# An ifftshift of an 8192 x 8192 matrix: from sixteen quadrant DMAs to sixty-four whole-row DMAs

## The chip, the cores and the metric

One core of one Trainium2 chip runs the kernel. The metric is the device time of one execution in microseconds (us). A profiled execution has a span too, from its first to its last recorded instruction; the time on the device is a little longer than the span.

## The reference

```python
def setup_inputs():
    return {
        "x": np.random.randn(8192, 8192).astype(np.float32),
    }

def reference(x: np.ndarray) -> np.ndarray:
    return np.fft.ifftshift(x)
```

Both sides are even, so the shift is by half in each direction: output element (r, c) is input element ((r + 4096) mod 8192, (c + 4096) mod 8192). Nothing is computed; the four quadrants change places diagonally. The matrix has 268.4 MB, which are read once and written once. A row has 32 KiB, half a row 16 KiB.

## The kernel before

The kernel has no tiles and no compute. It moves the data from DRAM to DRAM by DMAs that SyncE (SP) issues, and SP issues nothing else. `quads` (lines 23 to 28) lists for each quadrant of the output its rows and columns and the rows and columns of the input that belong there. The outer loop (line 33) goes over the four quadrants, top left, top right, bottom left, bottom right; the inner one (line 36) cuts each into four pieces of 1024 rows. So there are 16 DMAs, each of 1024 half rows, 16 MiB.

In each DMA both sides have the same pattern: 1024 runs of 16 KiB, one run every 32 KiB, so that every other 16 KiB of both matrices is skipped. The skipped halves belong to another quadrant and are moved by a DMA four places later or earlier. Each DMA reports its end by 16 increments of its semaphore, and the packets of the trace lie on 16 DMA engines. If the 1024 rows are dealt to the engines in equal runs of neighbouring rows, an engine has 64 rows of each DMA, and the pieces of neighbouring engines begin 64 x 32 KiB = 2 MiB apart.

The order is that of the program: SP issues the DMAs one after the other on its one queue. The framework hands out eight semaphores for these DMAs in turn, so the ninth DMA and each after it waits until the DMA eight places earlier has landed. No two DMAs touch the same output bytes, and there is no other dependence. At the end SP waits for the last DMAs, and a closing barrier (recorded at line 70) ends the program. The four memsets recorded at line 59 belong to the framework.

Of the kernel before, what the change touches and what calls it, by code (L numbers as in the profile page):

```python
# [1 line left out]

# [4 lines left out]


@with_exitstack  # L10
def kernel(
    ctx: ExitStack,
    tc: tile.TileContext,
    x: bass.AP,
    out: bass.AP,
):
    nc = tc.nc

    R, C = x.shape
    hr = R // 2  # L20
    hc = C // 2

    quads = [
        ((0, hr), (0, hc), (hr, R), (hc, C)),
        ((0, hr), (hc, C), (hr, R), (0, hc)),
        ((hr, R), (0, hc), (0, hr), (hc, C)),
        ((hr, R), (hc, C), (0, hr), (0, hc)),
    ]

    engines = [nc.sync]  # L30
    nsplit = 4
    k = 0
    for (or0, or1), (oc0, oc1), (ir0, ir1), (ic0, ic1) in quads:
        rows = or1 - or0
        step = rows // nsplit
        for s in range(nsplit):
            a = s * step
            b = a + step
            eng = engines[k % len(engines)]
            k += 1  # L40
            eng.dma_start(
                out=out[or0 + a : or0 + b, oc0:oc1],
                in_=x[ir0 + a : ir0 + b, ic0:ic1],
            )


# [1 line left out]
_INS = ['x']  # L48
_OUTS = [((8192, 8192), 'float32')]


def kernel(**inputs):
    import numpy as _np
    import concourse.bacc as _bacc
    import concourse.tile as _tile
    from concourse import mybir as _mybir
    from concourse.bass_utils import run_bass_kernel_spmd as _run

    nc = _bacc.Bacc("TRN2", target_bir_lowering=False, num_devices=1)  # L59
    arrays, args = {}, []  # L60
    for name in _INS:
        a = _np.ascontiguousarray(inputs[name])
        if a.dtype.kind in "iu":
            a = a.astype(_np.int64)
        arrays[f"in_{name}_dram"] = a
        args.append(nc.dram_tensor(f"in_{name}_dram", a.shape, _mybir.dt.from_np(a.dtype), kind="ExternalInput").ap())
    for i, (shape, dtype) in enumerate(_OUTS):
        dt = _mybir.dt.from_np(_np.dtype(dtype))
        args.append(nc.dram_tensor(f"out_{i}_dram", shape, dt, kind="ExternalOutput").ap())
    with _tile.TileContext(nc) as tc:  # L70
        kernel(tc, *args)
    r = _run(nc, [arrays], core_ids=[0])
    got = tuple(r.results[0][f"out_{i}_dram"] for i in range(len(_OUTS)))
    return got[0]
```

## Time and profile before

| | |
|---|---|
| median of 4 runs | 814.69 us (813.1 to 816.67) |
| the profiled execution, time | 814.51 us |
| the profiled execution, span | 812.7 us |
| DMAs issued | 16, of 16384 KB each |
| DMA packets | 16640: 16384 of data and 256 short ones |
| bytes under way | 268.44 MB read, 268.44 MB written |
| compute engines | POOL 0.2 us, all others nothing |

The profile has no compute to read. What remains is the DMA part: a line of tenths that says how busy the core's 16 DMA engines were in each of 40 slices of the span, a line with the rate in each slice (counted once per byte moved, though each byte is read and written), the sum over the queue, and the DMA issues with their median time from issue to landing. 16384 data packets for 268.44 MB are packets of 16 KiB: each run of half a row is one packet. The 256 short ones are 16 for each DMA, the semaphore increments.

### The profile page before, as it was taken

The numbers are of one execution on the slowest core, as the hardware profiler recorded it, in microseconds if no ns is written. First come the engines' busy times: TensorE is split into PE (matmuls) and PEld (weight loads), VectorE is DVE, ScalarE is ACT, GpSimd is POOL, SyncE is SP. The second block draws the span as 40 slices with busy tenths as digits, with TensorE's granted clock in tenths as the row PEclk, the third lists the DMA queues.
The fourth block names the chain that finished last, engine by engine and source line by source line (L and its number), as shares of the span: only waits on it lengthen the run. The fifth ranks groups of instructions, "written<-read, shape, count | busy, mean of one in ns | idle before, by whom it ended". The sixth has DMA issues, their size and how long they took to land. (4 is left out here: it accounts for less than half of the span.)

```text
span 812.7 us, 61 instructions
## 1 busy us (share of the span) xinstructions
POOL 0.2 (0%) x4
## 2 busy tenths in 40 slices
POOL 0000000000000000000000000000000000000000
DMA  9999999999999999999999999999999999999998
GB/s 297 327 314 330 331 334 323 333 323 333 332 335 326 337 333 334 331 335 340 331 333 335 331 335 328 335 334 331 331 333 336 338 333 332 334 335 335 331 336 295
DMA packets 16640, 268.44 MB, mean 330 GB/s; under 512 B 256, under 2 KB 256, under 8 KB 256
## 3 DMA queue, kind: packets, MB, share of 16 engines
q1 hardware_dynamic: 16640, 268.44, 99.2%
HBM read 268.44 MB, written 268.44 MB: 661 GB/s over the span
## 5 line engine op out<-in xcount | busy, mean ns | idle before, releaser
L59 POOL MEMSET const-uint8-127<- 128x1 uint8 x1 | 0.1, 103 | 0.0
L59 POOL MEMSET const-bfloat16-1.0<- 128x1 bf16 x1 | 0.1, 102 | 0.0
L59 POOL MEMSET const-float32-1.0<- 128x1 f32 x1 | 0.1, 100 | 0.0
L59 POOL MEMSET const-float32-0.0<- 128x1 f32 x1 | 0.1, 99 | 0.2 <-issue 0.2
## 6 DMA issues: line engine op xcount, KB each, us to landing
out_dram<-in_x_dram SPq DMA_DIRECT2D x16, 16384.0 KB, 157.7
```

Of the source, the lines that this page charges most:

```text
L59: nc = _bacc.Bacc("TRN2", target_bir_lowering=False, num_devices=1)
```

## The change

The loop over quadrants is replaced by a loop over blocks of 128 output rows, in order from the top. One DMA writes a block whole: 128 rows of 32 KiB, 4 MiB without a gap. It reads the 128 input rows that lie half the matrix away. Within a row the source begins at the second half (`+ hc`) and steps back by half a row (`[-hc, 2]`) to the first. There are 64 DMAs instead of 16, all still issued by SP in one line.

```diff
+ROWS_PER_DMA = 128
...
-    engines = [nc.sync]
-    nsplit = 4
-    k = 0
-    for (or0, or1), (oc0, oc1), (ir0, ir1), (ic0, ic1) in quads:
-        rows = or1 - or0
-        step = rows // nsplit
-        for s in range(nsplit):
-            a = s * step
-            b = a + step
-            eng = engines[k % len(engines)]
-            k += 1
-            eng.dma_start(
-                out=out[or0 + a : or0 + b, oc0:oc1],
-                in_=x[ir0 + a : ir0 + b, ic0:ic1],
-            )
+    for row in range(0, R, ROWS_PER_DMA):
+        src = (row + hr) % R
+        nc.sync.dma_start(
+            out=bass.AP(
+                out.tensor,
+                out.offset + row * C,
+                [[C, ROWS_PER_DMA], [hc, 2], [1, hc]],
+            ),
+            in_=bass.AP(
+                x.tensor,
+                x.offset + src * C + hc,
+                [[C, ROWS_PER_DMA], [-hc, 2], [1, hc]],
+            ),
+        )
```

An access pattern lists, from the outside in, pairs of step and count, in elements. In the built program the destination stands as 256 runs of 4096 elements one behind the other, the source as 128 rows of two runs with a step of -4096. The contiguous run stays half a row, 16 KiB, on both sides. With equal shares of neighbouring rows an engine now has 8 rows of a DMA, 16 runs, and the pieces of neighbouring engines begin 8 x 32 KiB = 256 KiB apart. The eight semaphores are handed out as before, so from the ninth DMA on each waits for the one eight places earlier; 56 of 64 DMAs have such a wait, where 8 of 16 had it.

More of the change, by code (lines that the diff above doesn't have):

```diff
@@ L21 @@
     hc = C // 2
[L23 to L28, printed above, removed]
-    engines = [nc.sync]
-    nsplit = 4
-    k = 0
-    for (or0, or1), (oc0, oc1), (ir0, ir1), (ic0, ic1) in quads:
-        rows = or1 - or0
-        step = rows // nsplit
-        for s in range(nsplit):
-            a = s * step
-            b = a + step
-            eng = engines[k % len(engines)]
-            k += 1
-            eng.dma_start(
-                out=out[or0 + a : or0 + b, oc0:oc1],
-                in_=x[ir0 + a : ir0 + b, ic0:ic1],
-            )
+    for row in range(0, R, ROWS_PER_DMA):
[12 more added lines that the diff above has]
+        )
 _INS = ['x']
```

## The prediction

> **What bounds the kernel now.** I read the page first: the slices, the queue and the HBM line.
>
> ```profile
> DMA  9999999999999999999999999999999999999998
> GB/s 297 327 314 330 331 334 323 333 323 333 332 335 326 337 333 334 331 335 340 331 333 335 331 335 328 335 334 331 331 333 336 338 333 332 334 335 335 331 336 295
> ...
> q1 hardware_dynamic: 16640, 268.44, 99.2%
> HBM read 268.44 MB, written 268.44 MB: 661 GB/s over the span
> ```
>
> The 16 DMA engines are busy in every slice and 99.2% of the span. Only the first and last slice fall below 310 GB/s, because they hold the start and the end. So no gap can be closed; time changes only if a packet takes longer or shorter.
>
> Next, SP's line and its waits, to see whether issuing ever limits the transfers.
>
> ```profile
> L41 SPq DMA_DIRECT2D out_dram<-in_x_dram x16: 578/49485/95256, 0.7 to 653.6; - x16
> ...
> DMA to landing us min/median/max: 54.9/157.7/200.0
> ```
>
> The shortest issue took 578 ns; the median of 49,485 ns is SP held back by a full queue, since a DMA of 16.8 MB takes 16.8/330 = 50.8 us to move. Landing 157.7 us after the issue means about three DMAs queued ahead. SP is far ahead of the data; the last issue begins at 653.6 us.
>
> Third, windows of 5 us around the place where one DMA gives way to the next. The second DMA's 16 increments arrive from 105.2 to 106.6 us.
>
> ```profile
> core 0: us, POOL busy (x), PEclk, DMA share, GB/s
> 95.00:100.00 5.00, 0.00 (x0) 1.00 0.97 318
> 100.00:105.00 5.00, 0.00 (x0) 1.00 1.01 338
> 105.00:110.00 5.00, 0.00 (x0) 1.00 1.00 328
> 110.00:115.00 5.00, 0.00 (x0) 1.00 0.98 328
> ```
>
> The window with the handover, 105 to 110, has a share of 1.00 and 328 GB/s, like its neighbours: a boundary between DMAs costs nothing visible.
>
> Last, the packet records themselves. The 16384 data packets of 16 KiB took 787 ns in the mean, 740 in the median, 608 at the least; 32% took 615 or less, 1% over 1341. Packets follow each other on an engine with about 2 ns between. So an engine alone moves a packet in 608 ns, and the other 179 ns are what reading and writing with 15 others costs. The span adds up: 1024 packets per engine x 0.787 = 806.0, about 2.3 us until the first packet, 1024 x 2 ns = 2.3 between packets, the rest of 2.1 for uneven ends and the closing barrier: 812.7. I write it as 1024 m + 6.7.
>
> One more reading carries the estimate. I put the data packets in order of start and cut them into 1024 rounds of 16 (the 16 engines finish each DMA within 2 us, so a round is nearly one packet of each). Numbering the rounds by eights, the mean duration by place in the eight is 758, 777, 767, 795, 820, 806, 786, 789 ns, each with a standard error of 6.4 ns; the first and the second half of the run show the same rise in the middle. Eight rounds are 8 x 32 KiB = 256 KiB of address in each engine. So what a packet costs depends on where the engines stand in the matrix, by about 4% each way.
>
> **The change part by part.** *SP's issues, 16 to 64.* At the two unhindered durations, 578 and 652 ns, 64 issues are 37 to 42 us of SP, against 800 us of transfer: hidden behind the queue. The new period is 4.19 MB/330 GB/s = 12.7 us, twenty times an issue. If that cover were gone the worst is 48 x 0.65 = 31 us.
>
> *The waits.* From the ninth DMA on each issue waits for the DMA eight earlier; queued behind it on SP are only the later DMAs, and the engines are the ones who would wait for those. While it waits seven DMAs, 7 x 12.7 = 89 us, are queued. The queue held about three DMAs of 65 packets per engine, and eight of 17 packets (136) are fewer than that. Price 0. Without that cover each later DMA would show the time from issue to first packet, 2.09 - 0.73 = 1.36 us.
>
> *Semaphore packets.* 48 more per engine at 9 ns, on the path: +0.4 us.
>
> A page that speaks against the change, weighed here: the Trainium skill, "DMA: Bandwidth & Descriptors", section "Anatomy of one DMA", puts a fixed cost of about 2.0 us on each DMA (fitted on the GpSimd path), mostly the receipt of the last write; 48 more in series would be +96 us by an estimate from that page. The handover window at 1.00 share does not show it, so the sum has 0.4 us here.
>
> *The first and the last packet.* The first DMA still needs about 1.4 us to its first packet, and the last packets still end unevenly by a packet or so. 0.
>
> *The address pattern.* This is the only large term. Packet size (16 KiB), count (16384), engines (16) and bytes stay. What changes: an engine writes its piece without gaps instead of every other 16 KiB; the two halves of a row are moved in neighbouring packets, where before they were four DMAs, some 200 us, apart; and the engines stand 256 KiB apart, no longer 2 MiB. The trace of before has no packet with the new pattern, so m is bounded by its own places: if all went as in the best place of the eight, m = 758, if all as in the worst, 820. The outer rows are the means of eight successive rounds, 736 at the lowest and 894 at the highest, 764 to 811 for nine tenths of them. The floor of 608 for every packet would need 16 engines that do not disturb each other, which no stretch approaches.
>
> I take m = 777. That is the shortest mean over one of the 16 DMAs (the thirteenth and the fifteenth; the sixteen run from 813 in the first down to 777), so a value this stream holds for 50 us. I choose the fast side because each difference removes something that can only cost: skipped bytes between two runs, and a second visit to the same rows. I do not go to 758, because 661 GB/s of reads and writes may leave little room.
>
> A page on the same point: in "DMA: Bandwidth & Descriptors", section "Latency and other measured facts", the Trainium skill reports copies between HBM tensors at 207 GB/s with a row pitch of 512 KiB, 164 at 2 MiB and 214 with a padded pitch. Read as the distance between engines, which its rows need not be, it would free 1 - 164/214 = 23% by an estimate from that page, some 625 us. The trace's 330 GB/s per direction at 2 MiB is above every one of its figures, so I do not use it.
>
> *The sum.* 1024 x 0.777 = 795.6, + 6.7 + 0.4 = 802.7 span. The profiled execution took 814.51 for a span of 812.7, 1.8 more, and the median is 0.2 above that: 804.7 us, 10 below 814.69.
>
> **The rivals.** *Slower by collisions in the new pattern (0.36).* The place is each packet's 179 ns over the floor. For it: the duration moves with the position inside 256 KiB, and that is now exactly the distance between engines and the length of a piece, so all 16 start each DMA in the same place; an engine that is one packet ahead is 16 KiB away and no longer 32; and within one DMA of before all reads lie in one half of the rows and all writes in the other, which the new order mixes. Against: before too all engines started alike, 2 MiB being a multiple of 256 KiB. Price: the mean of the four slower places, (820 + 806 + 786 + 789)/4 = 800 ns, gives 819.2 + 7.1 + 2.0 = 828 us; the worst place 820 gives 849. It decides from m = 789 on, where 1024 m is 2 us above today.
>
> *No change (0.08).* If the 661 GB/s are the limit whatever the order, only the 0.4 us remain: 815 us. For it: the 100-us rates from 200 us on are all 332 to 335. Against: the places in the eight.
>
> *The queue runs dry between smaller DMAs (0.05).* If the wait on the eighth DMA back left the engines without work, 48 x 1.36 = 65 us: 880. The 89 us of queue speak against it.
>
> *The change doesn't do what it says (0.01).* If source and destination of different shape were dealt to 8 engines, 2048 packets x 608 ns = 1245 us at least. If the contiguous destination became packets of 32 KiB, half of the 2.3 us between packets would go: 813.
>
> **How the numbers follow.** The forecast, faster, has 0.50; its own range is 785 (m = 758) to 812. About 0.3%, 2.4 us, is what a measurement of this kernel can tell from no change. Faster 0.50, within 0.3% 0.08, slower 0.36 + 0.05 + 0.01 = 0.42. The range goes up to 849 (m = 820) and leaves out 0.08 of the collision rival, the dry queue and the wrong engines; down it goes to 775, about halfway between 785 and the 763 that the fastest eight rounds (736) would give, and leaves out 0.04.
>
> **What would show it.** 17408 packets (16384 of 16 KiB, 1024 short) show that packets and engines are unchanged. A DMA share of 99% with the rate alone moved, near 334 GB/s, confirms that only m moved; a share below 97% with dips every 12.7 us would be the dry queue. Landing about 8 x 12.6 = 100 us after issue shows the depth. The rise in the middle of the eight rounds should change its shape. The prediction is wrong if m comes out above 787, and wrong in kind if the time lies in gaps.

## The result and the profile after

The changed kernel takes 814.52 us (median of 52 runs, 813.02 to 815.86), the kernel before 815.58 us (median of 79 runs). The ratio is 0.9985 with a 95% interval of 0.9976 to 0.9994: faster by 0.15%, inside the 0.3% that the prediction calls no change. The forecast was 804.7 us. The profiled execution has a span of 812.2 us, against 812.7.

The page of the changed kernel, much the same lines as were shown of before:

```profile
DMA  8999999999999999999999999999999999999998
GB/s 304 329 330 332 332 328 334 332 334 327 334 334 335 330 330 339 328 333 334 330 333 332 334 332 333 332 331 339 330 326 333 335 331 332 331 338 329 330 338 290
DMA packets 17408, 268.44 MB, mean 331 GB/s; under 512 B 1024, under 2 KB 1024, under 8 KB 1024
...
q1 hardware_dynamic: 17408, 268.44, 99.6%
HBM read 268.44 MB, written 268.44 MB: 661 GB/s over the span
```

The engines are as full as before, and the joint rate of reads and writes is again 661 GB/s. There are 17408 packets, 16384 of data and 64 x 16 short ones, so the packets are what they were; the order of the addresses and the number of DMAs are new.

SP's line in the same trace, with the time of one issue and from issue to landing:

```profile
L31 SPq DMA_DIRECT2D out_dram<-in_x_dram x64: 596/11820/28919, 0.7 to 730.1; - x64
...
DMA to landing us min/median/max: 15.3/80.0/94.5
```

An unhindered issue still takes 0.6 us. The median of 11.8 us is the full queue again, close to the 12.7 us that a DMA of 4.19 MB needs. Landing after 80 us means that some six DMAs lie in the queue. It never runs dry.

The packet records say where the forecast went. A data packet took 789 ns in the mean (787 before), the floor is 608 again, and 28% took 615 or less (32% before). What is not packets, span minus 1024 means, fell from 6.6 to 4.1 us. Put in rounds of 16 and numbered by eights, the means are 782, 774, 796, 786, 782, 786, 806, 801 ns, each with a standard error of about 5 ns: the pattern over the eight places is flatter and lies elsewhere, and its mean is nearly the same. So, as far as one trace of each kernel tells, the single packets did react to the new addresses, and the sum did not.

### The profile page after: what moved, and what is told of

It reads as the page before. It is cut to its first block, busy times and chain, and to the rows that moved or that the text cites. A ratio compares the mean times of both kernels' runs of the same rounds, so it can differ in the third digit from the quotient of the medians.

```text
span 812.2 us, 109 instructions
## 1 busy us (share of the span) xinstructions
POOL 0.2 (0%) x4
## 2 busy tenths in 40 slices
DMA packets 17408, 268.44 MB, mean 331 GB/s; under 512 B 1024, under 2 KB 1024, under 8 KB 1024
## 3 DMA queue, kind: packets, MB, share of 16 engines
q1 hardware_dynamic: 17408, 268.44, 99.6%
```

## Experiments

Every ratio is against runs of the kernel before on the same chip. Those took 823.7 to 826.5 us in the median, 1% more than the runs above, so the times below are not compared with those above.

The traces name neither the engine nor the address of a packet. Every distance between engines below rests on what was assumed for the kernel before: that the entries of a DMA's outermost dimension, here rows, are dealt to the engines in equal runs of neighbours. The runs with 8, 12 and 14 engines fit that, since the row count sets how many engines work, but they don't show which rows each engine gets.

### Half of the change at a time

`quad_128rows` keeps the quadrants and takes over the small DMAs:

```diff
-    nsplit = 4
...
+        for step in [128] * 32:
```

> One part of the change alone: DMAs of 128 rows (engines 256 KiB apart, 128 DMAs of 2 MiB), but quadrants as before, every other 16 KiB. Theory 'shared limit' (16 engines together get about 661 GB/s of reads plus writes, whatever the order; a packet takes what is left to it): within 0.5% of before, ratio 0.995 to 1.005. Rival 'two effects cancel' (the near halves gain, the short distance between engines loses): slower, ratio 1.01 or more, since here only the loss is in. Small DMAs leave the queue dry: over 850 us and a DMA share under 97%.

Measured: 1.0001 [0.9973, 1.0030]. 128 DMAs instead of 16 and 256 KiB between engines instead of 2 MiB cost nothing.

`whole_1024rows` keeps the whole rows and takes back the distance of 2 MiB between engines, with 1024 rows a DMA:

```diff
-ROWS_PER_DMA = 128
+ROWS_PER_DMA = 1024
```

> The other part alone: whole rows with the source stepping back, but 1024 rows a DMA, so that the engines stand 2 MiB apart as before (8 DMAs of 32 MiB). Shared limit: ratio 0.995 to 1.005. Two effects cancel: faster, ratio 0.99 or less, since here only the gain is in.

Measured: 1.760 [1.747, 1.773]. Neither theory allowed for this: whole rows alone are not faster but slower by three quarters. So it isn't two effects of like size that cancel either; the two parts of the change don't add.

`engines_32KiB_apart` deals the rows of a quadrant out in turn:

```diff
+                    [[C, 16], [16 * C, step // 16], [1, hc]],
```

> Quadrants and DMA sizes of before, but the rows are dealt out in turn: neighbouring engines stand one row, 32 KiB, apart, and an engine steps 512 KiB from packet to packet. Shared limit: ratio 0.99 to 1.01. A pattern-sensitive packet time (places in the eight worth 758 to 820 ns): a change of more than 1.5% one way or the other.

Measured: 1.0004 [0.9964, 1.0043]. Its packets have a mean of 806 ns in a profiled execution with a span of 832.8 us (834.6 us on the device, 1% above the median of this run), and 35% of them took 615 ns or less. Sixty-four times less distance shows no change.

`engines_16MiB_apart` uses the other end. It exchanges the halves of the rows and leaves out the shift by rows:

```diff
+                    [[R // 16 * C, 16], [C, 64], [1, hc]],
```

> Half rows as before, but an engine has 512 neighbouring rows of the whole matrix, so that neighbouring engines stand 16 MiB apart on both sides. The shift by rows is left out (an output row holds the same input row with its halves exchanged). Shared limit whatever the order: ratio 0.99 to 1.01. Pattern-sensitive packet time: slower by 5% or more, the packet mean over 830 ns, the floor unchanged at 608.

Measured: 2.619 [2.602, 2.637], the packet mean 2079 ns, the floor still 608. So order can cost a great deal, though here the missing row shift differs as well as the distance. The rates that several orders share, near 330 GB/s per direction, look like a ceiling, and the bad orders fall below it; the next runs test that.

### What the ceiling is: fewer engines, and one direction alone

The pieces are cut so that the rows of nearly all of them divide by 8, 12 or 14 and by nothing larger up to 16, for example for twelve:

```diff
+        for step in [996, 996, 996, 996, 108, 4]:
```

> Quadrants as before, cut into pieces of 1016 and 1048 rows, which can be dealt evenly to 8 engines and not to 16. Shared limit: 8 engines are under it, each packet comes near the floor of 608 to 611 ns, so 2048 x 0.611 + 7 = about 1258 us. Rival 'own pace' (a copy from DRAM to DRAM costs an engine 787 ns a packet whatever the others do): 2048 x 0.789 + 7 = about 1623 us.

> Quadrants as before, nearly all in pieces of 996 rows, which can be dealt to 12 engines. Shared limit: 12 engines at the floor would move 12 x 26.8 = 322 GB/s, just under the 330 seen, so 1365 packets each; between 840 us (all at the floor) and 900 us, packet mean 611 to 650 ns. Own pace: 1365 x 0.789 = 1084 us.

> Pieces of 1022 rows, dealt to 14 engines. At the floor they would move 375 GB/s. Shared limit: the 330 GB/s hold with two engines fewer, 812 to 830 us, packet mean about 690 to 700 ns in place of 787. Own pace: 1170 x 0.789 + 7 = 930 us.

Measured: 1249.5 us with 8 engines (1.514 [1.505, 1.523]), 837.9 with 12 (1.015 [1.011, 1.019]), 870.6 with 14 (1.055 [1.050, 1.059]). Windows of the three traces, in the order 8, 12, 14 engines; the last two columns are the busy share of 16 engines and the rate:

```profile
100.00:200.00 100.00, 0.00 (x0) 1.00 0.50 216
400.00:500.00 100.00, 0.00 (x0) 1.00 0.50 216
```

```profile
100.00:200.00 100.00, 0.00 (x0) 1.00 0.75 321
400.00:500.00 100.00, 0.00 (x0) 1.00 0.76 324
```

```profile
460.00:480.00 20.00, 0.00 (x0) 1.00 0.88 325
820.00:840.00 20.00, 0.00 (x0) 1.00 0.50 216
840.00:860.00 20.00, 0.00 (x0) 1.00 0.50 215
```

With 8 engines each packet takes 611 ns (99.9% of them 615 or less), with 12 the mean is 612: twelve engines move 642 GB/s of reads and writes over the span without getting in each other's way, and are 1.5% slower than sixteen. Engines 13 to 16 add next to nothing. That is the ceiling, and it is not an engine's own pace. (The time itself, 837.9 us, came out just under the expected 840 to 900.)

Fourteen engines reach the same 325 GB/s but end later than twelve; the expectation of 812 to 830 us missed. The ceiling is not shared evenly there: of the 14 increments of the second DMA, 6 arrive at 93 to 95 us and 8 at 117. The lucky six run through all that SP has queued and then stand idle, at the end and several times before it. The page shows the dips:

```profile
DMA  7888888888788888867888888688888868878754
...
q1 hardware_dynamic: 16640, 268.44, 81.5%
```

Fourteen engines at work throughout would give 87.5%. In windows of 5 us the share falls to 0.53 or less for 100 us in all after the start, 820 to 865 us among them. There only eight are at work, at 216 GB/s, and all their packets after 824 us take 611 ns: it was the others that had slowed them, not something of their own. By an estimate from these numbers 100 us at 216 in place of 325 GB/s lose 34 us, about the 33 us by which fourteen engines are slower than twelve. Why it is just these six that are served first no run shows.

`read_only` lands the blocks in on-chip memory and writes nothing out; `write_only` writes one tile of zeros to every block. The edit of read_only:

```diff
+        t = pool.tile([128, 2, hc], mybir.dt.float32)
...
-            out=bass.AP(
...
+            out=t[:, :, :],
```

> All writes to the output are left out: the blocks of the changed kernel are read into tiles of on-chip memory. 16 engines, the same 268.44 MB read with the same source pattern. Shared limit on the sum of reads and writes in DRAM: with half the DRAM traffic the packets come to the floor, 1024 x 0.611 + 7 = about 633 us, up to 660. Own pace or a limit in the engines: 780 us or more.

> All reads of the input are left out: one tile of on-chip memory is filled with zeros once and written to every block of the output, 268.44 MB in 64 DMAs. If the limit of 330 GB/s is one on the sum of reads and writes in DRAM, writes alone come to the engines' floor: about 633 us plus the fill of the tile, under 670. If it is a limit on writes, they stay at 330 GB/s: about 812 us plus the fill.

Measured: 632.8 and 636.8 us, ratios 0.767 [0.762, 0.771] and 0.772 [0.768, 0.775]. The pages, read_only first:

```profile
q1 hardware_dynamic: 17408, 268.44, 100.0%
HBM read 268.44 MB, written 0.00 MB: 426 GB/s over the span
```

```profile
DMA packets 9216, 268.44 MB, mean 423 GB/s; under 512 B 1024, under 2 KB 1024, under 8 KB 1024
...
HBM read 0.00 MB, written 268.44 MB: 423 GB/s over the span
```

In one direction 16 engines run close to their floor: 615 ns a packet when reading; the writes went out as 8192 packets of 32 KiB, 1219 ns each. The ceiling of 330 GB/s belongs to neither direction alone. It shows only with both at once, and then stands at about 650 to 661 GB/s together. The Trainium skill gives one HBM domain about 716 GB/s ("HBM Reference", section "Specifications (TRN2)"); 661 is 92% of that. No run here shows whether the ceiling sits in the memory or on the way to it, nor whether it counts the sum of reads and writes or is one of copies from DRAM to DRAM.

### What costs below the ceiling

`whole_1024rows` and before both have engines 2 MiB apart, yet one takes 1.76 times the other. What could matter is the distance together with what differs between the two: the gapless pieces, the mixing of the two halves of a row, and the step back. Eight runs take these apart, and a ninth looks at the changed kernel for a remainder.

`whole_1008rows` cuts the blocks at 1008 rows (four of them and a rest of 64 in each half of the matrix), `whole_512rows` and `whole_256rows` at 512 and 256; `quads_same_half` leaves out the exchange of halves:

```diff
-        ((0, hr), (0, hc), (hr, R), (hc, C)),
+        ((0, hr), (0, hc), (hr, R), (0, hc)),
...
```

> Whole rows in blocks of 1008 rows, so that the engines stand 63 rows, 2 MiB less 32 KiB, apart; all else as in the run with 1024 rows (1.76 times the time of before). If that run was slow because neighbouring engines stood exactly 2 MiB apart: ratio 0.99 to 1.03. If it was slow because of long gapless pieces or of the mixing of halves as such: ratio 1.5 or more.

> Whole rows in blocks of 512 rows, engines 1 MiB apart, between the changed kernel (256 KiB, shared limit reached) and 1024 rows (2 MiB, 1.76 times). If the loss comes from 2 MiB alone: ratio 0.99 to 1.02. If it grows with the distance: 1.05 to 1.5.

> Whole rows in blocks of 256 rows, engines 512 KiB apart. If the loss grows steadily with the distance (1.00 at 256 KiB, 1.26 at 1 MiB, 1.76 at 2 MiB): 1.05 to 1.15. If it begins at 1 MiB: 0.99 to 1.02.

> Before, with the exchange of the two halves of a row left out (only the row shift remains): engines 2 MiB apart, every other 16 KiB, but reads and writes of a DMA lie in the same half of the rows. If before escapes the loss at 2 MiB because its reads and its writes keep to different halves: ratio 1.2 or more. If it escapes it because a packet steps 32 KiB and not 16: ratio 0.99 to 1.02.

Measured: whole_1008rows 1.022 [1.018, 1.027] (two runs), whole_512rows 1.256 [1.251, 1.262], whole_256rows 1.041 [1.037, 1.045], quads_same_half 0.9986 [0.9943, 1.003]. Taking 63 rows in place of 64 between engines removes nearly all of the 76%, so it is the distance of exactly 2 MiB, at least in this order. The loss shrinks as the distance is halved: 1.76 at 2 MiB, 1.26 at 1 MiB, 1.04 at 512 KiB (a little under what was expected), nothing at 256 KiB. And keeping reads and writes in different halves is not what saves before.

`quads_back_step` leaves before as it is but lets the source take each pair of rows in reverse; `plain_1024rows` moves whole rows without exchanging halves; `quads_two_level` has pairs of rows on both sides that step forward; `whole_1024_dst_back` puts the back step on the destination. One line of each edit, in this order: the source of quads_back_step, the source of plain_1024rows, both sides of quads_two_level, the destination of whole_1024_dst_back:

```diff
...
+                    [[2 * C, step // 2], [-C, 2], [1, hc]],
...
+            in_=x[src : src + 1024, :],
...
+                    [[4 * C, step // 4], [C, 2], [1, hc]],
...
+                [[C, ROWS_PER_DMA], [-hc, 2], [1, hc]],
```

> Quadrants with 1024 rows a DMA as before, every other 16 KiB, engines 2 MiB apart, but the source takes the rows of each neighbouring pair in reverse order (steps of -32 KiB, then +96 KiB); in the output the rows of each pair are exchanged. If the back step costs: ratio 1.2 or more. If the gapless 16 KiB step is what costs at 2 MiB: ratio 0.99 to 1.02.

> Blocks of 1024 whole rows with the exchange of the halves left out (only the row shift remains): both sides gapless, in runs of 64 KiB, engines 2 MiB apart, no back step. If the gapless pieces at 2 MiB cost: ratio 1.2 or more. If it takes the back step: 0.99 to 1.02, the shared limit with packets four times as long.

> Quadrants in blocks of 1024 rows, each by two DMAs that take rows 4i, 4i+1 and rows 4i+2, 4i+3: pairs in both patterns, engines 2 MiB apart, every step forward. If any pattern of pairs costs at 2 MiB: ratio 1.2 or more. If it takes the back step: ratio 0.99 to 1.03.

> Whole rows, 1024 rows a DMA, but the source runs forward and the destination steps back over the halves. If a back step on either side costs: ratio about 1.76 as with the source. If it is a matter of reading backward: ratio 0.99 to 1.05.

Measured: quads_back_step 1.507 [1.501, 1.513], plain_1024rows 0.9967 [0.9945, 0.9990], quads_two_level 0.9973 [0.9953, 0.9992], whole_1024_dst_back 1.760 [1.752, 1.768]. Windows of quads_back_step, then of quads_two_level:

```profile
300.00:400.00 100.00, 0.00 (x0) 1.00 1.00 221
600.00:700.00 100.00, 0.00 (x0) 1.00 0.99 218
```

```profile
400.00:500.00 100.00, 0.00 (x0) 1.00 1.00 328
```

The DMA share is the same in both, so only the packets grew: 1199 ns in the mean against 795. Gapless pieces that go forward are fast (plain_1024rows, though its 4096 packets have 64 KiB each, so it differs in packet size too), pairs that go forward are fast, and a step back at 2 MiB is slow: on either side without gaps, and with gaps on the source, the one side tried. What the runs don't separate is the step back itself from its consequence, that reads and writes no longer run through their addresses in the same order; a kernel in which both sides step back together was not tried. Why this hurts only at distances of 512 KiB, 1 MiB and 2 MiB, and hardly at 2 MiB less 32 KiB, stays open too. The packets give one hint: numbered by fours, the rounds of whole_1024rows have means of 1144, 1259, 1639 and 1543 ns, a cycle of 64 KiB in each engine.

`whole_64rows` is the changed kernel with blocks of 64 rows, so that the engines stand 128 KiB apart.

> The changed kernel with 64 rows a DMA, engines 128 KiB apart, 128 DMAs. If the changed kernel stands at the shared limit: ratio 0.995 to 1.003, as it did (0.9985). If it still pays a part of the loss that grows with the distance: 0.99 or less.

Measured: 0.9989 [0.9974, 1.0004], like the changed kernel's 0.9985. At 256 KiB no part of that loss shows any more: halving the distance once more brings nothing, as it should if both stand at the ceiling.

## Why the prediction was wrong, point by point

- **The bound.** Right: engines busy throughout, time moves only with the packets. 99.2% became 99.6%.
- **Issues, waits, handovers, semaphore packets.** Right in their sum. 64 DMAs cost nothing visible, nor do the 128 of quad_128rows. The fixed cost of about 2.0 us a DMA that the Trainium skill states ("DMA: Bandwidth & Descriptors", section "Anatomy of one DMA"), fitted on another path and weighed in the prediction as +96 us for 48 more in series, shows in no run with this queue. Landing came after 80 us, not 100.
- **The address pattern, the step that failed: "I take m = 777".** Measured was 789 on the trace. 1024 x 12.1 ns = 12.4 us too little, of which 3.0 came back because the rest was 4.1 us instead of 7.1; together the 9.4 us by which the span of 812.2 missed the sum (802.75 before rounding). The reason given for the fast side, that each difference removes something that can only cost, took part of the 179 ns over the floor for losses that a better order could save. The runs with 8 and 12 engines show what they are: sixteen engines ask for more than the 650 to 661 GB/s of reads and writes that are to be had, and the mean is what is left to each, 16 engines x 16.4 KB / 333 GB/s = 787 ns. No order tried with 16 engines was faster than before by more than 0.33% (plain_1024rows, 0.9967); that none could be isn't shown.
- **The places in the eight.** They were real in this trace, and read for more than they can say. The stream does run faster and slower with them: from one round of 16 to the next it is 761 ns at the fastest place and 825 at the slowest. But every engine passes through all eight, and no run shows why they differ, so nothing said that a new order would keep to the good ones. Its own places average 789 ns. The prices at the edges of the range, m = 758 and 820, came from such places. No mean of 16 engines over a whole run with packets of 16 KiB was below 787 ns.
- **No change, at 0.08.** This is what happened, by the very limit that the rival named, at 815 us. The evidence named for it was steady rates of 332 to 335 GB/s from 200 us on. A steady rate in one order couldn't prove the same limit for another, but neither could the places in the eight, and they were given far more weight. A run with fewer engines would have told.
- **Collisions, at 0.36.** That an order can be slower is true, and by far more than the rival's 828 to 849 us: up to 1.76 times at 2 MiB. Whether collisions are the reason no run shows, and the place was wrong. The rival feared the short, equal distance of 256 KiB; the runs show the reverse, that with a step back only the distances of 512 KiB, 1 MiB and 2 MiB cost (1.04, 1.26 and 1.76 times), and 256 KiB nothing. Choosing 128 rows a DMA, and not 1024, is what kept the change from being a large loss.
- **The page on row pitch.** The Trainium skill ("DMA: Bandwidth & Descriptors", section "Latency and other measured facts") has copies lose with a pitch of 2 MiB. Read as the distance between engines it didn't hold at 2 MiB for forward orders (before, plain_1024rows). At 16 MiB, a pitch that the page doesn't list, 124 GB/s were left. The page reports that a pitch of 4 MiB padded by 4 KiB restores the rate; the nearest thing here is whole_1008rows, with a distance shorter by 32 KiB: 319 GB/s instead of 186.

## What to carry to other kernels

Where engines are busy all the time, first ask whether their packets are slow or whether they share a ceiling: a run with fewer engines tells, because under a ceiling the packets fall to their floor and the time hardly moves. At the ceiling no order tried here gained more than 0.33%, and a worse one cost up to 2.6 times. If a DMA has to step back within a row, keep the share of one engine small (here 256 KiB or less), or its length off a power of two (63 rows in place of 64, 1.02 times).

## What the runs showed of the hardware that was not expected

- Twelve of sixteen DMA engines copy DRAM to DRAM within 1.5% of the time of all sixteen; fourteen are slower than twelve (870.6 against 837.9 us), because six of them get ahead and then stand idle, while eight alone reach 216 GB/s.
- A step back of 16 KiB on one side of a copy, harmless with engines 256 KiB apart (0.9985), takes 1.76 times as long at 2 MiB. One of 32 KiB, tried at 2 MiB alone, takes 1.51 times.
- Engines 16 MiB apart take 2.6 times as long without any step back, in a run that also leaves out the shift by rows.
